# Row tiles transposed by VectorE in 32-row blocks, from quarter-row loads, in place of crossbar transposes

## The chip, the cores and the metric

The kernel runs on one core of a Trainium2 chip. Five engines work side by side, each through its own queue in the order in which its instructions were written: TensorE (PE; its weight loads are listed apart as PEld), VectorE (DVE), ScalarE (ACT), GpSimd (POOL) and SyncE (SP), which here only issues transfers. Semaphores tie the queues together. Matmul results land in PSUM, which has eight banks; GpSimd cannot reach it. The metric is the device time of one execution in microseconds (us). The median of two runs before is 370.06 us (369.67 and 370.45).

## The reference

x has 8 x 1024 rows of 768 float32 numbers, the weight matrix is 768 x 2304. Each row is divided by its root mean square, multiplied by gamma, and multiplied with the weights:

```python
def reference(x, gamma, w_qkv, eps):
    rms = np.sqrt(np.mean(x ** 2, axis=-1, keepdims=True) + eps)
    x_norm = x / rms * gamma
    return np.matmul(x_norm, w_qkv).astype(np.float32)
```

The output is 8 x 1024 x 2304 float32, 75.5 MB, x is 25.2 MB, the weights are 7.1 MB.

## The kernel before, in words

The 8192 rows are 64 tiles of 128 rows. TensorE contracts over partitions, so a tile of x must lie with its 768 columns on the partitions: six blocks (KO = 6) of 128 columns.

Tiles 0 to 3 take a plain way. x is cast to bfloat16 (`cast`), turned by TensorE (`tr`), copied out of PSUM (`cp`) and multiplied with the weights (`mm`, six matmuls of 512 columns for each output piece). The row factor 1/rms comes in when the result is taken out (`evac`). The weights are multiplied with gamma and cast in the meantime (`conv`). `gamma_in` turns gamma itself by a tiny float32 matmul (L482).

Tiles 4 to 63 are taken in pairs, p = 2 to 31: two row tiles by 768 output columns (c = 0, 1, 2) are a 2 x 2 by 2 x 2 block product, done with seven products in place of eight (Strassen's scheme in Winograd's form). The halves of the contraction are the first and last three of the six blocks of columns. The pieces are:

- `load_x`: one transfer for a tile, 3 KB for each partition.
- `pstat`, `prms`, `precip`: ScalarE squares a tile and adds along the row (L567, an ACTIVATE and a read of the accumulator); one root (L571) and one reciprocal (L576) serve a pair.
- `pcast` (L581): VectorE multiplies by 1/rms and casts to float16.
- `pxbar` (L585): a crossbar transpose, issued by SyncE, gives the tile `xT`.
- `osum` (L599): four sums and differences of half tiles for each pair, on GpSimd but for the first ones.
- `quad`, `tsum`: the eight weight operands in float16 for each c, made once, scaled by a bound on the column block (`bound`, `fold`, `bound_tr`, `bound_top`, `bound_all`, `scales`).
- `product` (L619): three matmuls of 384 columns. Seven products for each p and c go into three PSUM banks a, b, c.
- `hold` (L628 on ScalarE, L626 on VectorE), `join` (L637, VectorE) and `last` (L641, ScalarE): holds copy a partial sum out of a bank so that a further product can be added on top of it in the same bank; joins add a bank to a held part and write the output tile `ot`; last writes the fourth quarter. Product 6 goes into bank a after hold "p1" has read product 1; product 3 into bank c after hold "p5".
- `pstore` (L647): the output of a tile's 768 columns goes to memory.

The order is written out by hand. Each entry has a due time; all entries are sorted by it and issued in that order, so the due time sets the place in every engine's queue and nothing else. PLAN lists the first part: the weights, tiles 0 to 3, and pairs 2 to 11. HEAD_END (135.62) is the due time at which pair 12 begins. From pair 12 on the order is regular: one slot is three matmuls (SLOT = 0.4875 us), a column c takes seven slots, a pair 21. `when(u, ...)` places an operation u slots after the column's start; products 1, 5, 2, 6, 3, 7, 4 stand at 0, 1, 2, 4, 5, 10, 13, so the last two fall between those of the next column. Loads, square sums, casts and transposes of a pair stand many slots ahead of its first product, and are placed differently for even and odd pairs.

Tiles come from pools of a fixed number of buffers: nine for x, four for casts, ten for xT, twelve for outputs of 1024 columns, eight PSUM banks. An operation that wants a buffer waits until the earlier user is done with it.

Of the kernel before, what the change touches and what calls it, by code (L numbers as in the profile page):

```python
# [15 lines left out]
HEAD_END = 135.62  # L16
# [3 lines left out]
    (0.000, "load_x", 2), (4.040, "cast", 2, "DVE"), (4.041, "load_x", 0), (5.030, "cast", 0, "DVE"),  # L20
    (5.031, "stat", 2), (5.530, "recip", 2), (5.531, "gamma_in"), (5.532, "idle", 6, 512), (5.533, "tr", 2),
    (5.670, "tr", 0), (6.230, "cp", 0, "DVE"), (6.231, "stat", 0), (6.440, "cp", 2, "ACT"), (6.441, "load_x", 1),
    (6.442, "load_w", 3), (6.820, "cast", 1, "DVE"), (7.460, "tr", 1), (7.461, "load_w", 4),
    (7.480, "conv", 3, 4, "DVE"), (8.141, "conv", 4, 5, "DVE"), (8.142, "mm", 2, 0, "4"), (8.143, "load_w", 2),
    (8.801, "conv", 2, 3, "DVE"), (8.802, "load_w", 0), (8.803, "load_x", 3), (8.804, "cp", 1, "ACT"),
    (9.371, "bound", 0, 1, "DVE"), (9.372, "mm", 0, 0, "4"), (9.373, "mm", 2, 0, "5"), (9.374, "load_w", 1),
    (9.375, "mm", 0, 0, "5"), (9.376, "mm", 1, 0, "5"), (9.377, "mm", 1, 0, "4"), (9.574, "mm", 0, 0, "3"),
    (9.575, "load_w", 7), (9.576, "load_w", 5), (9.790, "mm", 1, 0, "3"), (11.111, "cast", 3, "DVE"),
    (11.112, "load_w", 6), (11.113, "stat", 1), (11.114, "conv", 0, 0, "ACT"), (11.115, "mm", 2, 0, "3"),
    (11.116, "conv", 0, 1, "POOL"), (11.117, "mm", 1, 0, "01"), (11.393, "mm", 0, 0, "01"), (11.394, "stat", 3),  # L30
    (11.395, "load_w", 9), (11.825, "tr", 3), (11.826, "conv", 1, 2, "DVE"), (13.092, "conv", 7, 4, "ACT"),
    (13.093, "conv", 7, 5, "POOL"), (13.094, "mm", 1, 0, "2"), (13.095, "mm", 2, 0, "012"), (13.205, "mm", 0, 0, "2"),
    (13.932, "mm", 2, 512, "45"), (14.364, "mm", 1, 512, "45"), (14.365, "load_w", 8), (14.413, "conv", 5, 1, "POOL"),
    (17.054, "conv", 9, 2, "POOL"), (17.055, "bound", 0, 0, "DVE"), (17.734, "conv", 9, 3, "POOL"),
    (17.735, "cp", 3, "DVE"), (17.736, "evac", 2, 0, "ACT"), (17.737, "mm", 0, 512, "54"),
    (17.738, "conv", 5, 0, "ACT"), (17.739, "mm", 3, 512, "45"), (18.414, "conv", 8, 0, "POOL"),
    (18.415, "mm", 2, 512, "01"), (18.416, "mm", 1, 512, "01"), (18.417, "recip", 1), (18.418, "evac", 1, 0, "DVE"),
    (18.419, "recip", 3), (18.420, "conv", 6, 3, "ACT"), (18.421, "conv", 6, 2, "DVE"),
    (18.422, "bound", 1, 0, "ACT"), (18.423, "load_w", 10), (18.424, "mm", 0, 512, "01"),
    (18.425, "mm", 0, 512, "23"), (18.426, "mm", 1, 512, "23"), (18.427, "mm", 2, 512, "23"),  # L40
    (18.428, "mm", 3, 512, "01"), (18.429, "evac", 1, 512, "ACT"), (18.430, "bound", 0, 2, "DVE"),
    (18.431, "recip", 0), (18.432, "fold", 0), (18.714, "conv", 8, 1, "ACT"), (19.494, "bound", 1, 1, "ACT"),
    (19.495, "bound_tr", 0), (19.496, "evac", 0, 0, "DVE"), (19.497, "mm", 2, 1024, "23"),
    (19.498, "mm", 0, 1024, "23"), (19.499, "bound_top", 0), (19.665, "bound_all", 0), (19.785, "mm", 2, 1024, "01"),
    (19.786, "load_x", 5), (21.094, "pstat", 5), (21.095, "mm", 3, 1024, "01"), (21.096, "evac", 0, 512, "DVE"),
    (21.097, "mm", 1, 1024, "01"), (21.098, "scales", 0), (21.099, "quad", 0, "b12", "DVE"),
    (21.100, "conv", 10, 5, "POOL"), (21.101, "conv", 10, 4, "POOL"), (22.064, "bound", 1, 2, "ACT"),
    (22.065, "mm", 0, 1024, "01"), (22.066, "quad", 0, "b22", "DVE"), (22.067, "load_w", 11),
    (22.068, "mm", 2, 1024, "45"), (22.069, "mm", 3, 1024, "45"), (22.535, "quad", 0, "b11", "DVE"),
    (23.275, "conv", 11, 0, "DVE"), (23.276, "load_x", 4), (23.705, "tsum", 0, "t3", "DVE"), (23.706, "load_w", 13),  # L50
    (24.405, "fold", 1), (24.406, "conv", 13, 5, "POOL"), (24.407, "pstat", 4), (24.408, "mm", 3, 512, "23"),
    (24.409, "mm", 0, 1024, "45"), (24.410, "mm", 1, 1024, "23"), (24.555, "evac", 3, 512, "DVE"),
    (24.556, "load_w", 15), (24.634, "conv", 11, 1, "ACT"), (24.635, "mm", 3, 1024, "23"),
    (24.636, "mm", 3, 0, "012345"), (25.215, "evac", 2, 512, "DVE"), (25.216, "load_x", 6), (25.396, "bound_tr", 1),
    (25.397, "prms", 2), (25.875, "precip", 2), (25.876, "mm", 1, 1024, "45"), (25.948, "mm", 2, 1536, "01"),
    (25.949, "load_x", 7), (25.950, "conv", 13, 4, "POOL"), (26.380, "mm", 2, 1536, "45"),
    (26.381, "conv", 15, 3, "POOL"), (26.382, "load_w", 12), (26.383, "bound_top", 1), (26.384, "conv", 15, 5, "DVE"),
    (26.455, "tsum", 0, "t1", "DVE"), (26.812, "bound_all", 1), (26.813, "conv", 15, 4, "ACT"),
    (26.932, "mm", 0, 1536, "01"), (26.933, "evac", 2, 1024, "ACT"), (26.934, "evac", 3, 1024, "ACT"),
    (27.363, "mm", 1, 2048, "345"), (27.691, "mm", 0, 1536, "45"), (27.692, "evac", 1, 1024, "ACT"),  # L60
    (27.693, "pcast", 4), (27.705, "pcast", 5), (27.706, "load_w", 14), (28.608, "conv", 12, 3, "POOL"),
    (29.635, "conv", 14, 0, "POOL"), (29.636, "tsum", 0, "t2", "DVE"), (29.637, "mm", 3, 1536, "45"),
    (29.638, "mm", 3, 1536, "01"), (29.639, "pxbar", 5), (29.640, "mm", 1, 1536, "01"), (29.641, "pstat", 6),
    (29.642, "pstat", 7), (29.643, "scales", 1), (29.644, "evac", 3, 0, "DVE"), (29.645, "mm", 1, 1536, "45"),
    (29.849, "mm", 3, 2048, "345"), (29.850, "conv", 12, 2, "ACT"), (30.177, "mm", 2, 2048, "345"),
    (30.334, "prms", 3), (30.335, "bound", 2, 1, "DVE"), (30.504, "mm", 3, 1536, "23"),
    (30.584, "conv", 14, 1, "ACT"), (31.615, "precip", 3), (31.616, "evac", 0, 1024, "ACT"),
    (31.617, "conv", 14, 2, "POOL"), (31.618, "mm", 1, 1536, "23"), (31.619, "mm", 2, 2048, "012"),
    (31.715, "osum", 2, "s1", "DVE"), (31.716, "mm", 1, 2048, "012"), (32.085, "pcast", 6),
    (32.086, "quad", 1, "b11", "ACT"), (32.814, "evac", 2, 2048, "ACT"), (32.815, "pcast", 7),  # L70
    (32.816, "quad", 0, "b21", "POOL"), (32.817, "mm", 3, 2048, "012"), (32.818, "pxbar", 4),
    (33.185, "osum", 2, "s2", "DVE"), (33.186, "load_x", 8), (33.187, "load_x", 10), (33.188, "mm", 0, 1536, "23"),
    (33.189, "mm", 2, 1536, "23"), (33.645, "osum", 2, "s4", "POOL"), (33.646, "quad", 1, "b21", "DVE"),
    (33.647, "pxbar", 6), (33.648, "product", 2, 0, 2), (33.649, "evac", 3, 2048, "ACT"),
    (33.701, "product", 2, 0, 1), (34.245, "evac", 1, 2048, "DVE"), (34.246, "load_x", 9), (34.445, "pxbar", 7),
    (35.215, "quad", 1, "b12", "POOL"), (35.216, "evac", 2, 1536, "DVE"), (36.485, "quad", 1, "b22", "POOL"),
    (36.486, "product", 2, 1, 1), (36.487, "product", 2, 1, 2), (36.488, "bound", 2, 0, "ACT"),
    (36.489, "evac", 3, 1536, "DVE"), (36.490, "hold", 2, 0, "a", "p1", "ACT"), (36.491, "load_x", 11),
    (36.492, "load_x", 12), (36.535, "load_x", 13), (36.536, "hold", 2, 1, "a", "p1", "DVE"),
    (36.537, "bound", 2, 2, "ACT"), (36.538, "product", 2, 0, 5), (36.539, "join", 2, 0, 0, 0, "b", "p1"),  # L80
    (36.540, "product", 2, 0, 6), (36.541, "product", 3, 0, 1), (37.205, "product", 3, 1, 2),
    (37.206, "join", 2, 1, 0, 0, "b", "p1"), (37.294, "hold", 2, 0, "c", "p5", "ACT"),
    (37.794, "evac", 1, 1536, "ACT"), (37.795, "fold", 2), (37.796, "store", 2, 1, 1024, 1024),
    (37.797, "tsum", 1, "t1", "DVE"), (38.394, "evac", 0, 1536, "ACT"), (38.465, "osum", 2, "s3", "DVE"),
    (38.466, "bound_tr", 2), (38.994, "hold", 2, 0, "a", "u2", "ACT"), (38.995, "product", 2, 0, 3),
    (38.996, "tsum", 1, "t2", "DVE"), (38.997, "product", 2, 1, 5), (39.494, "hold", 2, 1, "c", "p5", "ACT"),
# [215 lines left out]
def kernel(  # L302
# [115 lines left out]

    HALF = {"A": (0, 4), "B": (4, KO)}

    def tr_half(t, h):
        k0, k1 = HALF[h]
# [315 lines left out]
```

## Time and profile before

| | |
|---|---|
| median of two runs | 370.06 us |
| profiled execution, whole | 371.79 us |
| its span, first to last instruction | 369.5 us |
| mean granted TensorE clock | 0.995 of full speed |
| operand sums on GpSimd (L599), 114 in three groups | mean 929 to 948 ns for 128 x 384 |
| square sums on ScalarE (L567), 60 | 837 ns and a 191 ns accumulator read |
| casts on VectorE (L581), 60 | 690 ns mean, 612 median |
| holds on ScalarE / VectorE | 213 of 580 ns / 57 of 616 ns |
| joins (L637), 270 | 613 ns |
| products' matmuls (L619), 1890 | listed with 326 ns, pipelined; one starts every 0.163 us |
| their weight loads | 98 ns |
| crossbar transposes, issue on SyncE | 60, median 1390 ns |
| other issues on SyncE, median | output stores 384 ns, x loads 550 ns |
| an x load / a transpose / an output store, from issue to landing | 5.9 / 5.2 / 5.2 us |
| packets | 89295, of which 52390 are under 512 B |

A group's line gives line, engine, operation, output and inputs by their names in the program, shape and count; then the busy time, the mean of one in ns, and the idle time before them with what ended it. A wait line gives who waited, for whom, the sum in us, the number of times and the longest. A line of the chain or the timeline gives start and length in us. A window's line gives the stretch, then busy time and count for each engine, the granted clock, the busy share of the transfer engines and GB/s. Durations of neighbouring instructions on one engine overlap, so what one costs is read from the starts.

### The profile page before, as it was taken

To read this page: it belongs to the slowest core of one execution; us is meant where nothing else is said; L and a number is where in the kernel's file an instruction comes from. 1 tells how busy PE (TensorE), PEld (TensorE's weight loads), DVE (VectorE), ACT (ScalarE), POOL (GpSimd) and SP (SyncE) were. 2 spreads that over 40 slices of the span, in tenths; PEclk is the share of its full clock that TensorE was granted. 3 is DMA by queue.
4 is the path that set the end of the run, shared out by engine and by line. 5 is a ranking of instruction groups with operands and counts; after the bars stand their busy time and mean duration, and the time that the engine had idled before them with its cause. 6 is when DMAs were issued, how large, how long until landed. Compare 5 with 4: busy or idle time off the path is not lost.

```text
span 369.5 us, 6553 instructions
## 1 busy us (share of the span) xinstructions
PE 345.3 (93%) x2045; PEld 200.2 (54%) x2047; DVE 261.5 (71%) x484; ACT 247.5 (67%) x502; POOL 126.2 (34%) x141
## 2 busy tenths in 40 slices
PE   5998999799989989889999999999999999999995
PEld 3444555465545545545656566565656656556663
DVE  3899978587557857657868576776868676776653
ACT  4798988476558767447585765757575776745453
POOL 0257734324214433333043342507070613343000
PEclk9999999999999999989999999999999999999999
DMA  7998999989999999999999999999999999786656
GB/s 256 392 387 218 268 398 267 333 264 326 265 394 365 342 323 350 274 364 353 390 328 410 293 402 347 403 300 391 330 382 312 359 335 360 286 259 244 248 227 245
DMA packets 89295, 119.98 MB, mean 325 GB/s; under 512 B 52390, under 2 KB 54188, under 8 KB 89260
## 3 DMA queue, kind: packets, MB, share of 16 engines
q1 hardware_dynamic: 89248, 119.56, 98.8%
q8 instruction: 16, 0.26, 0.3%
q14 instruction: 19, 0.16, 0.2%
q10 hardware_dynamic: 12, 0.00, 0.0%
HBM read 32.25 MB, written 75.50 MB: 292 GB/s over the span
## 4 chain that ended last, share of the span: by engine, by line
PE 59%; DMA 20%; ACT 7%; issue 5%; DVE 3%; SPq 3%; POOL 1%; ACTq 0%; DVEq 0%; POOLq 0%
PE pm L619 59%; DMA out_dram<-ot 11%; DMA wq<-in_w_qkv_dram 7%; ACT sq L567 3%; DVE ot L637 2%; ACT pp L628 2%; SPq L370 2%; ACT ot L641 1%; DMA xT<-xb 1%; SPq L585 1%; DVE xb L581 1%; POOL wq L551 1%; POOL w_b L385 1%; ACT sq L509 0%; SPq L647 0%
## 5 line engine op out<-in xcount | busy, mean ns | idle before, releaser
L619 PE MATMUL pm<-wq,su 128*128 128x384 f16 x1080 | 207.1, 326 | 7.4 <-ACT pp L628 4.6
L637 DVE SCALAR_TENSOR_TENSOR ot<-pm,sc,pp 128x384 f32<-128x384 f32 x270 | 156.3, 613 | 70.5 <-PE pm L619 43.7
L628 ACT ACTIVATE pp<-pm,sc 128x384 f32<-128x384 f32 x213 | 121.1, 580 | 77.6 <-PE pm L619 76.1
L619 PE MATMUL pm<-wq,xT 128*128 128x384 f16 x810 | 161.8, 327 | 6.7 <-DVE ot L637 6.6
L619 PEld LDWEIGHTS <-su 128*128 128x128 f16 x1080 | 105.3, 98 | 80.8 <-issue 11.0
L619 PEld LDWEIGHTS <-xT 128*128 128x128 f16 x810 | 79.5, 98 | 62.1 <-issue 10.9
L599 POOL TENSOR_TENSOR su<-xT 128x384 f16<-128x384 f16 x55 | 50.9, 946 | 176.1 <-DMA xT<-xb 139.4
L641 ACT ACTIVATE ot<-pm,sc 128x384 f32<-128x384 f32 x90 | 51.8, 577 | 32.1 <-PE pm L619 27.9
L626 DVE TENSOR_SCALAR pp<-pm,sc 128x384 f32<-128x384 f32 x57 | 35.1, 616 | 23.2 <-PE pm L619 23.2
L567 ACT ACTIVATE sq<-x_t 128x768 bf16<-128x768 f32 x60 | 50.2, 837 | 0.5
L581 DVE TENSOR_SCALAR xb<-x_t,rstd 128x768 f16<-128x768 f32 x60 | 41.2, 690 | 1.1 <-DMA xT<-xb 0.5
L599 POOL TENSOR_TENSOR su<-su,xT 128x384 f16<-128x384 f16 x29 | 27.5, 948 | 12.5 <-DMA xT<-xb 9.9
L599 POOL TENSOR_TENSOR su<-xT,su 128x384 f16<-128x384 f16 x30 | 27.9, 929 | 3.8 <-DVE su L599 1.6
L449 PE MATMUL pm<-w_b,xT 128*128 128x512 bf16 (+1 forms) x118 | 25.7, 369 | 1.6 <-POOL w_b L385 1.2
L449 PEld LDWEIGHTS <-xT 128*128 128x128 bf16 x120 | 11.7, 100 | 13.2 <-issue 3.4
L385 POOL TENSOR_SCALAR w_b<-wq,g_sb 128x512 bf16<-128x512 f32 (+1 forms) x14 | 11.6, 837 | 20.0 <-DMA wq<-in_w_qkv_dram 20.0
L567 ACT ACTIVATION_READ_ACCUMULATOR sq<-x_t 128x1 f32 x60 | 11.5, 191 | 0.0
L571 ACT ACTIVATE rms<-ssq,eps_sb 128x2 f32<-128x2 f32 x30 | 8.8, 292 | 0.2
L557 DVE TENSOR_TENSOR wq<-wq 128x1152 f16<-128x1152 f16 x11 | 8.1, 747 | 0.0
L506 DVE TENSOR_REDUCE bnd<-w_b 128x1 f32<-128x1536 bf16 x4 | 7.0, 1753 | 0.9 <-POOL w_b L385 0.4
L509 ACT ACTIVATE sq<-w_b 128x1536 bf16<-128x1536 bf16 x5 | 7.4, 1480 | 0.3
L383 ACT ACTIVATE w_b<-wq,g_sb 128x512 bf16<-128x512 f32 (+1 forms) x9 | 6.0, 669 | 1.9 <-DMA wq<-in_w_qkv_dram 1.8
(47 smaller groups left out, 67.2 us busy)
## 6 DMA issues: line engine op xcount, KB each, us to landing
out_dram<-ot SPq DMA_DIRECT2D x178, 384.0 KB, 5.2
x_t<-in_x_dram SPq DMA_DIRECT2D x64, 384.0 KB, 5.9
wq<-in_w_qkv_dram SPq DMA_DIRECT2D x10, 512.0 KB, 9.3
out_dram<-ot SPq DMA_DIRECT2D x8, 512.0 KB, 8.5
wq<-in_w_qkv_dram SPq DMA_DIRECT2D x4, 256.0 KB, 6.9
xT<-xb SPq DMA_TRANSPOSE x60, 5.2
wq<-in_w_qkv_dram SPq DMA_DIRECT2D x2, 384.0 KB, 9.8
out_dram<-ot SPq DMA_DIRECT2D x4, 192.0 KB, 2.3
```

The lines of the kernel that those rows point to most:

```text
L385: nc.gpsimd.tensor_scalar(out=o, in0=i, scalar1=g, scalar2=1.0, op0=mult, op1=mult)
L449: nc.tensor.matmul(out=PM[t, n0][:, :nl], lhsT=XT[t][:, ko, :], rhs=w_b[:, ko, n0:n0 + nl], start=(b == 1), stop=(b == KO))
L557: (nc.vector if eng == "DVE" else nc.gpsimd).tensor_tensor(out=new_quad(c, q), in0=i0, in1=i1, op=sub)
L567: nc.scalar.activation(out=sq, in_=X[t], func=AF.Square, accum_out=SS[p][:, t % 2:t % 2 + 1])
L571: nc.scalar.activation(out=r, in_=SS[p], func=AF.Sqrt, scale=inv_k, bias=eps_sb)
L581: nc.vector.tensor_scalar(out=XB[t], in0=X[t], scalar1=SS[t // 2][:, t % 2:t % 2 + 1], scalar2=None, op0=mult)
L599: (nc.vector if eng == "DVE" else nc.gpsimd).tensor_tensor(out=block(p, q), in0=block(p, x), in1=block(p, y), op=op)
L619: nc.tensor.matmul(out=PB[k][:, :CW], lhsT=block(p, a)[:, ko, :], rhs=WQ[c, b][:, ko, :], start=(first and ko == 0), stop=(ko == KO // 2 - ...
L626: nc.vector.tensor_scalar(out=o, in0=pb, scalar1=SC[c], scalar2=None, op0=mult)
L628: nc.scalar.activation(out=o, in_=pb, func=AF.Copy, scale=SC[c], bias=0.0)
L637: nc.vector.scalar_tensor_tensor(out=result(p, c, i, j), in0=PB[p, c, bank][:, :CW], scalar=SC[c], in1=PART[p, c, held], op0=mult, op1=add)
L641: nc.scalar.activation(out=result(p, c, 1, 0), in_=PB[p, c, "a"][:, :CW], func=AF.Copy, scale=SC[c], bias=0.0)
```

## The change: what it does

- x of tiles 4 to 63 comes as quarter rows (`load_g`): four transfers for each tile, packets of 768 B. On partition 32 g + i lie, side by side, the g-th quarters of rows i, 32 + i, 64 + i, 96 + i (index m).
- The square sums are taken for each quarter row: `pstat(t, h)` makes two of the four 192-column sums of a tile. The four quarters of a row lie on four partitions; `psum_k` adds them with one float32 matmul against a 0/1 matrix `same_row` for each pair, and hands the sums to all four partitions. `prms` and `precip` then work on eight columns.
- `pcast` is a multiplication of two tensors, on GpSimd but for two tiles in the first part.
- `pturn` is a VectorE transpose in 32 x 32 blocks. Two neighbouring float16 numbers are treated as one 32-bit word, so 384 words per partition give the whole tile. Partition q then holds columns 6 q to 6 q + 5 of all 128 rows, with the two numbers of a word next to each other: the weight operand that TensorE loads steps over every other half word.
- The weights are loaded to match (row 6 q + ko on partition q), gamma comes straight into that layout (`gamma_in` goes), the two halves of the contraction are the even and odd ko, and the first tiles' cast writes its columns in that order.
- Crossbar transposes, and some functions without a caller, are removed.
- PLAN is written anew: tiles 5 and 4 are loaded early, other operations change engine, HEAD_END is 142.52. In the regular part even and odd pairs now have the same offsets, and the hold "p5" of the third column is on VectorE too.

```diff
-HEAD_END = 135.62
+HEAD_END = 142.52
...
-    g6 = singles.tile([KO, P], f32)
-    nc.scalar.dma_start(out=g6, in_=gamma.rearrange("(ko p) -> ko p", p=P))
+    gam = singles.tile([P, KO], f32)
+    nc.scalar.dma_start(out=gam, in_=gamma.rearrange("(p ko) -> p ko", ko=KO))
...
+    row_sel = singles.tile([P, B], f32)
+    nc.vector.tensor_reduce(out=row_sel, in_=ident_f.rearrange("p (g i) -> p i g", g=G), axis=mybir.AxisListType.X, op=add)
+    same_row = singles.tile([P, P], f32)
+    nc.vector.tensor_copy(out=same_row.rearrange("p (g i) -> p g i", g=G), in_=row_sel.unsqueeze(1).to_broadcast([P, G, B]))
...
-    wv = w_qkv.rearrange("(ko p) n -> p ko n", p=P)
+    wv = w_qkv.rearrange("(p ko) n -> p ko n", ko=KO)
...
-        copy(eng, XB[t], X[t])
+        copy(eng, XB[t].rearrange("p (ko q) -> p q ko", ko=KO), X[t].rearrange("p (q ko) -> p q ko", ko=KO))
...
-        k0, n0 = KO // 2 * (q[1] == "2"), 2 * CW * c + CW * (q[2] == "2")
-        return w_b[:, k0:k0 + KO // 2, n0:n0 + CW]
+        s, n0 = int(q[1] == "2"), 2 * CW * c + CW * (q[2] == "2")
+        return w_b.rearrange("p (b s) n -> p s b n", s=2)[:, s, :, n0:n0 + CW]
...
-    def pstat(t):
+    def load_g(t):
+        X[t] = xin.tile([P, G, K // G], f32, name="x_t")
+        xs = xf[t * P:(t + 1) * P, :].rearrange("(m i) (g k) -> g m i k", i=B, g=G)
+        for m in range(G):
+            nc.sync.dma_start(out=X[t][:, m, :], in_=xs[:, m])
+
+    def pstat(t, h):
         p = t // 2
         if p not in SS:
-            SS[p] = stats.tile([P, 2], f32, name="ssq2")
-        sq = junk.tile([P, 2 * K], bf16, name="sq")[:, :K]
-        nc.scalar.activation(out=sq, in_=X[t], func=AF.Square, accum_out=SS[p][:, t % 2:t % 2 + 1])
+            SS[p] = stats.tile([P, 2 * G], f32, name="ssq2")
+        sq = junk.tile([P, 2 * K], bf16, name="sq")[:, :K // G]
+        for m in (2 * h, 2 * h + 1):
+            i = G * (t % 2) + m
+            nc.scalar.activation(out=sq, in_=X[t][:, m, :], func=AF.Square, accum_out=SS[p][:, i:i + 1])
+
+    def psum_k(p):
+        ps = psum.tile([P, 2 * G], f32, name="pm")
+        nc.tensor.matmul(out=ps, lhsT=same_row, rhs=SS[p], start=True, stop=True)
+        SS[p] = ps
...
-    def pcast(t):
-        XB[t] = xbp.tile([P, K], f16, name="xb")
-        nc.vector.tensor_scalar(out=XB[t], in0=X[t], scalar1=SS[t // 2][:, t % 2:t % 2 + 1], scalar2=None, op0=mult)
-
-    def pxbar(t):
-        XT[t] = xTp.tile([P, KO, P], f16, name="xT")
-        nc.sync.dma_start_transpose(out=XT[t], in_=XB[t])
+    def pcast(t, eng):
+        XB[t] = xbp.tile([P, G, K // G], f16, name="xb")
+        r = SS[t // 2][:, G * (t % 2):G * (t % 2 + 1)]
+        (nc.vector if eng == "DVE" else nc.gpsimd).tensor_tensor(
+            out=XB[t], in0=X[t], in1=r.unsqueeze(2).to_broadcast([P, G, K // G]), op=mult)
+
+    def pturn(t):
+        o = xTp.tile([P, H, P], f32, name="xT")
+        nc.vector.transpose(out=o.rearrange("p b (m i) -> p m b i", i=B),
+                            in_=XB[t].rearrange("p m k -> p (m k)").bitcast(f32).rearrange("p (m j b) -> p m b j", m=G, j=B))
+        XT[t] = o.rearrange("p b q -> p (b q)").bitcast(f16).rearrange("p (b q s) -> p s b q", s=2, q=P)
...
-                odd = p % 2
                 for i in range(2):
                     t = 2 * p + i
-                    when((-96, -110)[odd] + 7 * i, load_x, t)
-                    when((-64, -78)[odd] + 7 * i, pstat, t)
-                    when((-45, -57)[odd] + 4.5 * i, pcast, t)
-                    when((-42, -54)[odd] + 4.5 * i, pxbar, t)
-                when((-54.5, -68)[odd], prms, p)
-                when((-46, -58)[odd], precip, p)
+                    when(-72 + 7 * i, load_g, t)
+                    when(-46 + 7 * i, pstat, t, 0)
+                    when(-43 + 7 * i, pstat, t, 1)
+                    when(-30 + 7 * i, pcast, t, "POOL")
+                    when(-22.3 + 7 * i, pturn, t)
+                when(-33.5, psum_k, p)
+                when(-32.5, prms, p)
+                when(-31, precip, p)
...
-            when(2.1, hold, p, c, "c", "p5", "DVE" if c < 2 else "ACT")
+            when(2.1, hold, p, c, "c", "p5", "DVE")
```

## The prediction, made before any run of the change

> **What bounds the kernel now.** I read the page's busy times first, then the chain that ended last, then who waited for whom, and last the windows, in which matmuls can be counted and held against the written order.
>
> ```profile
> PE 345.3 (93%) x2045; PEld 200.2 (54%) x2047; DVE 261.5 (71%) x484; ACT 247.5 (67%) x502; POOL 126.2 (34%) x141
> ...
> PE 59%; DMA 20%; ACT 7%; issue 5%; DVE 3%; SPq 3%; POOL 1%; ACTq 0%; DVEq 0%; POOLq 0%
> ```
>
> TensorE is busy nearly throughout, yet 20% of the chain is transfers. The waits say where they come in:
>
> ```profile
> DVE ot L637 <- DMA out_dram<-ot: 19.5, 22, 2.9
> ...
> PE pm L619 <- DVE ot L637: 6.6, 9, 1.9
> ...
> PE pm L619 <- ACT pp L628: 4.6, 10, 0.5
> ```
>
> A join on VectorE waits until an old output tile has been stored; TensorE then waits for that join's bank. All 22 of these waits lie between 30 and 165 us. The windows (us, then busy time and count of TensorE, weight loads, VectorE, ScalarE, GpSimd, then clock, DMA share, GB/s):
>
> ```profile
> 0.00:65.00 65.00, 57.90 (x314) 30.60 (x317) 53.05 (x105) 53.66 (x101) 29.25 (x35) 1.00 0.98 313
> 0.00:150.00 150.00, 136.17 (x781) 76.17 (x784) 111.05 (x210) 110.84 (x221) 57.45 (x65) 1.00 1.02 321
> ...
> 190.00:320.00 130.00, 126.68 (x775) 75.54 (x774) 93.51 (x174) 88.28 (x189) 49.17 (x55) 1.00 1.06 349
> 340.00:350.00 10.00, 10.00 (x64) 5.99 (x62) 6.20 (x12) 5.20 (x11) 0.00 (x0) 1.00 0.61 243
> ```
>
> A run of 108 matmuls in the chain takes 17.73 us, so one takes 0.1626 us when nothing waits (the last one's 0.17 tail taken off). The plan has 775 matmuls before pair 12, the first pair of the regular part; 781 had run by 150 us, so pair 12 began at 149.0. Its due time was 135.62, and the first load goes out at 0.73: **12.7 us late**. At 65 us the kernel had run 314 matmuls, about where it was due at 62: 2 to 3 us late. So some 10 us were lost between 65 and 149, in the waits for stores. After pair 12, 2047 - 775 = 1272 matmuls need 206.8 us; the last ended at 365.6, so 9.8 us were lost there too, and 3.9 us of last evacuation and store make the span of 369.5.
>
> In the regular part (190 to 320) 775 matmuls take 130 us, 10.57 us for a pair's 63 where 10.24 would do: 0.3 us a pair. The chain shows why:
>
> ```profile
> 209.43 0.83 ACT L567 ACTIVATE sq<-x_t 128x768 bf16<-128x768 f32 x1
> 210.16 0.19 ACT L567 ACTIVATION_READ_ACCUMULATOR sq<-x_t 128x1 f32 x1
> 210.38 0.84 ACT L567 ACTIVATE sq<-x_t 128x768 bf16<-128x768 f32 x1
> 211.13 0.19 ACT L567 ACTIVATION_READ_ACCUMULATOR sq<-x_t 128x1 f32 x1
> 211.23 0.56 ACT L641 ACTIVATE ot<-pm,sc 128x384 f32<-128x384 f32 x1
> 211.69 0.57 ACT L628 ACTIVATE pp<-pm,sc 128x384 f32<-128x384 f32 x1
> ```
>
> Two whole sums of squares stand ahead of a last and a hold, and product 6 waits for that hold. Starts matter here, not durations: a hold frees ScalarE after 0.47, an accumulator read lets a hold follow after 0.10, another sum after 0.22.
>
> **What goes.** 60 crossbar transposes. In 340 to 350 there are none: 243 GB/s at a share of 0.61 is 398 GB/s at full share. In 190 to 320, 349 GB/s moved 45.4 MB; 25 tiles' transposes are 5.0 of it (0.197 MB each), the other 40.4 MB take 101.5 us at 398, and the remaining 28.5 us are 1.1 us a transpose. 60 of them are some 66 us of transfer time, 1.4 us each of SyncE's queue, too. The 41 us of casts on VectorE (L581) go as well, but for two.
>
> **What comes, per pair of 63 matmuls.**
>
> x in quarter rows: 8 issues where there were 2, packets of 768 B where there were 3 KB. SyncE: 8 x 0.43 + 6 stores x 0.38 = 5.7 us of 10.2, against 2 x 0.43 + 2 x 1.39 + 6 x 0.38 = 5.9 before; no gain, no loss. A tile's 393 KB take 1.0 us at 398 GB/s. No row has such packets: nothing more at one end, at the other twice the time (a transpose, with 870 small packets, pays 1.1 us for half the bytes). I take 1.3: of the 66 us that the transposes free, 60 x 0.3 = 18 are spent again; at twice the time 60 of them are, and the queue is as full as before.
>
> Sums of squares: 8 of 192 columns for 2 of 768. From the starts: 0.73 for 768 is 0.64 + 0.09, so 192 take 0.25, then 0.22 and 0.10 around the reads: 0.82 for each half tile, 3.3 us a pair against 1.7. With nine holds and lasts at 0.49 and the root, ScalarE fills 8.0 of 10.2 us. The halves are due apart (slots 3, 6, 17, 20 of 21). The tightest place: hold at slot 19.35, half tile, last, hold: 19.35 + 1.0 + 1.7 + 1.0 + 1.2 = 24.25, needed at 25. It fits by 0.4 us, so most of the 0.3 us stall should go. I put the loss S at 0.1 a pair, 3 us in all; bounds 0 and, as before, 0.3 (10 us).
>
> GpSimd: two casts of 768. Its subtractions take 0.93 for 384 columns and 2.94 for 1152, 2.6 ns a column: 1.94 each. With four operand sums 7.6 of 10.2; the second cast ends at about slot 5.5, its transpose stands at 5.7 in VectorE's order. VectorE: a transpose of 384 words has no row; 0.35 (the quickest 384-column sum) and 1.75 (a reduction of 1536) bound it, I take 0.62, as any one-input row of its size. Twelve joins and holds at 0.573, two transposes, a reciprocal: 8.3 of 10.2. The Trainium skill, "SBUF — State Buffer" (Door 1: The DMA port swizzle), says that reads which leave their 16-byte line pay; the transposes read words 12 bytes apart, and no run here shows it. By that rule VectorE would have perhaps 9.5 of 10.2, still hidden.
>
> Weight loads from xT now step over every other half word: 98 ns at best, twice that at worst, and 196 would stick out of a matmul's 163 by 33 ns, 27 us for 810. I take 98.
>
> **The new float32 product (psum_k)** is the one thing added to TensorE itself, 30 times. It stands in the queue ahead of all products and waits for the last square sum. Nearest rows (busy us, mean ns, idle before):
>
> ```profile
> L528 PE MATMUL pm<-btop,ones 1*128 1x1 bf16 x3 | 0.5, 173 | 0.0
> ...
> L482 PE MATMUL pm<-ident_f,g 6*128 6x6 f32 x1 | 0.2, 241 | 2.3 <-DMA g<-in_gamma_dram 2.3
> ...
> L482 PEld LDWEIGHTS pm<-ident_f,g 6*128 6x128 f32 x1 | 0.2, 177 | 2.3 <-POOL ones L492 2.3
> ```
>
> L528's follower starts 0.11 after it (21.14, 21.25): the low end. The only float32 row, L482, takes 177 for weights and 241: 0.42 when nothing covers its weights, which is the case behind a wait; a full 128 x 128 product could be twice that, 0.84. I take 0.42. The plan already leaves 0.13 after ten of them. Net 30 x 0.42 - 10 x 0.13 = 11.3 us. The rule against this change is in "FP8 and Floating Point Precision" (TensorE Precision Notes): a true float32 product makes four passes. Four passes at the 0.163 of an ordinary matmul would be 0.65 and the total 7 us more; no row here shows it.
>
> Strided casts, the selector matrix and gamma by column touch only the first microseconds, under the wait for x (2.16 us of VectorE at 1.7 to 3.9): nothing, or 1 us, inside L below.
>
> **The sum.** The changed plan puts pair 12 at 142.52, with 789 TensorE instructions before it (12 of the 30 psum_k). Start 0.73: 143.25. After it 2076 - 789 - 18 = 1269 products' matmuls x 0.1626 = 206.3. Tail 3.9. Together 353.5. Lateness L of the first part: 2 to 3 us without the store waits, and more work on ScalarE: 4; bounds 0 and 12.7. 353.5 + 4 + 11.3 + 3 = **371.8** against the span of 369.5, 2.3 more. That execution took 371.79 in all, 1.7 over the median of 370.06; I add the 2.3 to the median: **372.4**. The plan's later start and the float32 products eat what the transfers give.
>
> **Rivals.**
> - Faster, 0.22: psum_k at 0.11 (2.0), L 2, S 0: 353.5 + 4.0 = 357.5, 358 us. For it: L528; nothing else lies on TensorE. Against: float32.
> - Slower by ScalarE, 0.10: if reads of the accumulator cost their recorded 354 + 191 (1536 to 768 columns give 0.84 ns a column and 194 fixed), a half takes 1.1 us. The chain above then ends at 25.2, and the second half before psum_k at about slot 9.9 instead of 8.4, with psum_k at 9. That is 0.4 a pair in psum_k's wait and 0.3 in product 6: 22 us for S's 3, 391 us. It decides from 0.95 us a half.
> - The float32 product at its upper end, 0.12: 30 x 0.42 more, 385 us.
> - No relief, 0.07: small x packets refill the queue, L and S as before: 353.5 + 12.7 + 11.3 + 10, 388 us. The change then isn't what its transfers promise.
> - Strided weights (399 us) or a GpSimd cast at 4 us, from the 1371 ns row of 256 columns: 11.9 of 10.7 us a pair (406 us); 0.07.
> - My forecast 0.42, its own range 364 to 381.
>
> A measurement of this kernel tells some 2% (7.4 us) from no change. Faster 0.22. Slower: 0.10 + 0.12 + 0.07 + 0.07 and 0.06 from the forecast's upper end, 0.42. Within 0.36. For eight in ten the range takes in half of the fast case, the float32 and ScalarE ones: 359 to 391.
>
> **What to look for after.** No wait of L637 for stores; DMA share below 0.95 after 60 us; pair 12 near 147 (count 789); TensorE's idle time before psum_k and its span; 3.3 us of ScalarE starts per pair; PEld from xT still 98; GpSimd casts near 1.9. I am wrong if psum_k is far from 0.42, if holds wait behind square sums, or if the head loses more than 8 us again.

## The result, and the profile after

The changed kernel takes **486.27 us** (median of two runs, 484.96 to 487.59) against 370.06 before: a ratio of 1.314 (95% interval 1.298 to 1.330). The forecast was 372.4, with a range up to 391. Its profiled execution has a span of 483.2 us at a mean granted clock of 0.936. First the busy times and the chain that ended last, from the page of the changed kernel:

```profile
PE 379.0 (78%) x2106; PEld 213.7 (44%) x2106; DVE 293.8 (61%) x524; ACT 276.1 (57%) x824; POOL 208.7 (43%) x199
...
DMA 51%; PE 18%; SPq 17%; DVE 4%; issue 4%; ACT 4%; POOL 2%; DVEq 0%; ACTq 0%; POOLq 0%
```

TensorE fell from 59% of the chain to 18%. Transfers went from 20% to 51%, and SyncE's queue, which issues them, from 3% to 17%. The waits of the changed kernel (us in total, times, longest) say which transfers:

```profile
ACT sq L568 <- DMA x_t<-in_x_dram: 69.8, 97, 3.4
...
DVE ot L637 <- DMA out_dram<-ot: 46.1, 22, 7.7
...
PE pm L572 <- ACT sq L568: 35.7, 16, 2.7
```

The square sums now wait for x itself, which they hardly did before (all 60 of them together had 0.5 us of idle time in front). The joins' waits for stores, which were to go, grew from 19.5 to 46.1 us. A window of the regular part, with the columns of the windows shown for the kernel before, seems to contradict this:

```profile
190.00:320.00 130.00, 105.76 (x612) 60.93 (x610) 78.88 (x142) 77.15 (x244) 57.82 (x54) 0.96 0.61 229
```

612 matmuls instead of 775, and the transfer engines at a share of only 0.61, against 1.06 before. The kernel waits for transfers while, on average, four tenths of the transfer engines' time is free. That average is the trap of this case. The chain of the changed kernel (start, length, what) shows the loop that each pair runs through:

```profile
281.95 0.57 SPq L559
...
282.57 0.83 SPq L559
...
283.45 0.58 SPq L559
...
284.08 7.67 DMA x_t<-in_x_dram
...
291.83 0.10 ACT sq L568
...
292.33 0.39 PE pm L572 x2
292.72 2.53 PE pm L619 x9
...
295.27 0.59 ACT pp L628
...
296.01 0.57 SPq L559
```

The last quarter load of the pair, 98 KB, takes 7.67 us from its issue. After it come the square sum, psum_k, nine products, a hold, a store, and the next issue 14.06 us after the first. psum_k starts at 263.04, 278.08, 292.33, 306.59 and 320.83 us: **14.45 us a pair**, where 10.57 was measured before. The lower granted clock is not what lengthens a pair: of two neighbours, one at a clock of 0.88 and one at 0.98, both take 14.2 to 14.3 us:

```profile
292.33:306.59 14.26, 12.32 (x66) 6.90 (x66) 8.34 (x15) 8.16 (x27) 6.43 (x6) 0.88 0.59 222
306.59:320.83 14.24, 10.80 (x65) 6.30 (x65) 8.41 (x15) 8.27 (x27) 6.43 (x6) 0.98 0.58 220
```

### The profile page after: what moved, and what is told of

Read it like the earlier page. It is cut to its first block, busy times and chain, and to the rows that moved or that the text cites. A ratio compares the mean times of both kernels' runs of the same rounds, so it can differ in the third digit from the quotient of the medians.

```text
span 483.2 us, 7420 instructions
## 1 busy us (share of the span) xinstructions
PE 379.0 (78%) x2106; PEld 213.7 (44%) x2106; DVE 293.8 (61%) x524; ACT 276.1 (57%) x824; POOL 208.7 (43%) x199
## 4 chain that ended last, share of the span: by engine, by line
DMA 51%; PE 18%; SPq 17%; DVE 4%; issue 4%; ACT 4%; POOL 2%; DVEq 0%; ACTq 0%; POOLq 0%
DMA x_t<-in_x_dram 28%; DMA out_dram<-ot 20%; PE pm L619 17%; SPq L559 13%; DMA wq<-in_w_qkv_dram 3%; DVE ot L637 3%; SPq L647 2%; ACT sq L568 1%; PE pm L572 1%; POOL su L608 1%; ACT ot L641 1%; ACT pp L628 1%; SPq L469 1%; POOL xb L588 1%; DVE xT L593 1%
## 5 line engine op out<-in xcount | busy, mean ns | idle before, releaser
L619 PE MATMUL pm<-wq,su 128*128 128x384 f16 x1080 | 222.2, 342 | 26.5 <-DVE pp L626 13.1
L637 DVE SCALAR_TENSOR_TENSOR ot<-pm,sc,pp 128x384 f32<-128x384 f32 x270 | 157.8, 609 | 112.4 <-DMA out_dram<-ot 46.1
L619 PE MATMUL pm<-wq,xT 128*128 128x384 f16 x810 | 170.7, 339 | 14.0 <-DVE ot L637 13.8
L588 POOL TENSOR_TENSOR xb<-x_t,rstd 128x768 f16<-128x768 f32 x58 | 85.4, 1473 | 214.6 <-DVE rstd L582 166.1
L628 ACT ACTIVATE pp<-pm,sc 128x384 f32<-128x384 f32 x179 | 102.7, 576 | 75.4 <-PE pm L619 60.9
L568 ACT ACTIVATE sq<-x_t 128x192 bf16<-128x192 f32 x240 | 86.6, 361 | 73.1 <-DMA x_t<-in_x_dram 69.8
L626 DVE TENSOR_SCALAR pp<-pm,sc 128x384 f32<-128x384 f32 x91 | 55.8, 613 | 27.6 <-PE pm L619 27.4
L568 ACT ACTIVATION_READ_ACCUMULATOR sq<-x_t 128x1 f32 x240 | 45.1, 188 | 0.0
L593 DVE STREAM_TRANSPOSE xT<-xb 128x384 f32<-128x384 f32 x60 | 41.6, 694 | 0.0
L572 PE MATMUL pm<-ssq,same_row 128*128 128x8 f32 x60 | 11.3, 261 | 37.9 <-ACT sq L568 35.7
L572 PEld LDWEIGHTS pm<-ssq,same_row 128*128 128x128 f32 x60 | 10.4, 206 | 46.8 <-ACT sq L568 42.3
L400 POOL TENSOR_SCALAR w_b<-wq,gam 128x512 bf16<-128x512 f32 (+1 forms) x14 | 11.2, 810 | 31.3 <-DMA wq<-in_w_qkv_dram 31.3
```

What stands on the lines that cost most here:

```text
L568: nc.scalar.activation(out=sq, in_=X[t][:, m, :], func=AF.Square, accum_out=SS[p][:, i:i + 1])
L572: nc.tensor.matmul(out=ps, lhsT=same_row, rhs=SS[p], start=True, stop=True)
L588: (nc.vector if eng == "DVE" else nc.gpsimd).tensor_tensor(out=XB[t], in0=X[t], in1=r.unsqueeze(2).to_broadcast([P, G, K // G]), op=mult)
L593: nc.vector.transpose(out=o.rearrange("p b (m i) -> p m b i", i=B), in_=XB[t].rearrange("p m k -> p (m k)").bitcast(f32).rearrange("p (m j ...
L619: nc.tensor.matmul(out=PB[k][:, :CW], lhsT=block(p, a)[:, ko, :], rhs=WQ[c, b][:, ko, :], start=(first and ko == 0), stop=(ko == KO // 2 - ...
L626: nc.vector.tensor_scalar(out=o, in0=pb, scalar1=SC[c], scalar2=None, op0=mult)
```

## Why a small load takes so long: the theories

Every quarter load reads, in one transfer, a quarter of each row of a tile: from DRAM 4 column quarters, in each 32 rows (the g and i of `load_g`), in each 192 neighbouring numbers. The outermost dimension of that pattern has 4 entries. The load before had 128 rows outermost.

- **Theory N (narrow):** a transfer is spread over as many of the 16 transfer engines as its outermost dimension allows; here four, and always the same four. At the 398 GB/s of the prediction one engine moves 24.9 GB/s. x of a pair, 0.786 MB, keeps four engines busy for 7.9 us, and their part of the outputs (2.36 MB over 16 engines) for 5.9 us: 13.8 us a pair, while twelve engines are idle more than half the time.
- **Theory Q (queue):** eight issues a pair on SyncE, behind stores that wait for their data, send the loads off too late.
- **Theory P (packets):** packets of 768 B are slow by themselves.

The Trainium skill, "DMA: Bandwidth & Descriptors" (Why a DMA increments its semaphore by 16 and not by 1), states the rule that N needs: a transfer uses the largest number of engines, 16 at most, that divides the slowest dimension of both patterns, and from such a queue always the lowest-numbered ones. The prediction did not weigh it. The runs below agree with it for 2, 4 and 16; the trace does not number the engines.

## The experiments

**1. The same quarters, cut another way (e1_wide).** Each load now reads one column quarter of all 128 rows, with 32 rows outermost; bytes, packet size, number of issues and what lands where are the same.

```diff
-xs = xf[t * P:(t + 1) * P, :].rearrange("(m i) (g k) -> g m i k", i=B, g=G)
-for m in range(G):
-    nc.sync.dma_start(out=X[t][:, m, :], in_=xs[:, m])
+xs = xf[t * P:(t + 1) * P, :].rearrange("(m i) (g k) -> g i m k", i=B, g=G)
+for g in range(G):
+    nc.sync.dma_start(out=X[t][B * g:B * (g + 1), :, :], in_=xs[g])
```

> The changed kernel with one edit: a tile's four loads are cut by column quarter (32 partitions, all four row groups) and not by row group; same bytes, same 768 B packets, same four issues, same places. The source pattern then begins with a dimension of 32 and not of 4. Theory N (the quarter loads run on 4 of the 16 transfer engines, which carry 7.9 us of x and 5.9 us of outputs a pair): back to 360-385 us, about 10.6 us a pair. Theory Q (the loads stand too late in SyncE's queue, behind stores) and theory P (768 B packets are slow): above 470 us as before the edit.

Measured: **369.16 us**, ratio to the kernel before 0.9996 (0.9974 to 1.0019). From the page of this run, and its window of the regular part:

```profile
PE 346.5 (94%) x2104; PEld 206.6 (56%) x2106; DVE 291.8 (79%) x524; ACT 272.1 (74%) x824; POOL 209.1 (57%) x199
...
PE 85%; DMA 7%; DVE 3%; ACT 2%; SPq 1%; issue 1%; ACTq 0%; DVEq 0%
```

```profile
190.00:320.00 130.00, 130.00 (x817) 79.82 (x816) 103.20 (x188) 100.53 (x326) 80.69 (x76) 1.00 0.92 313
```

One rearrangement of the source takes away 117 us, and TensorE is busy 130.00 of 130 us. A quarter load lands after a median of 3.3 us. The joins' waits for stores, and the issues of quarter loads in the changed kernel and in this run (shortest, median and longest in ns):

```profile
DVE ot L637 <- DMA out_dram<-ot: 4.0, 6, 1.1
...
L559 SPq DMA_DIRECT2D x_t<-in_x_dram x240: 528/861/3063, 1.2 to 442.9; - x120
...
L559 SPq DMA_DIRECT2D x_t<-in_x_dram x240: 311/462/2302, 1.2 to 321.7; - x120
```

Packets of 768 B and eight issues a pair are harmless in this kernel: P and Q are out as the cause of the 486 us.

**2. Loads 24 slots earlier (e2_early).** The changed kernel, one number changed.

```diff
-when(-72 + 7 * i, load_g, t)
+when(-96 + 7 * i, load_g, t)
```

> The changed kernel with the regular part's loads 24 slots (11.7 us) earlier, nothing else. Theory Q: the loop from issue to landing to psum_k to the next issue is cut, the regular part runs at about 10.6 us a pair and the whole at 400-425 us (the first part keeps its loss). Theory N: four transfer engines still carry 13.8 us a pair, so 13.8 to 14.4 a pair and 465-490 us.

Measured: 486.02 us. The last load of a pair now goes off some 15 us ahead of its psum_k, 8.2 in the changed kernel, and a pair still takes 14.5 us. A loop that is only started too late would have gained; a full engine doesn't.

**3. Two engines instead of four (e9_two_engines).** The changed kernel with each quarter load issued as two halves, two column quarters each.

```diff
-nc.sync.dma_start(out=X[t][:, m, :], in_=xs[:, m])
+for h in range(2):
+    nc.sync.dma_start(out=X[t][64 * h:64 * h + 64, m, :], in_=xs[2 * h:2 * h + 2, m])
```

> The changed kernel with each quarter load issued as two halves, so that the outermost dimension of the source is 2 and not 4. Theory N (a load runs on as many transfer engines as that dimension has entries): x of a pair, 0.786 MB, on two engines at 24.9 GB/s each is 15.8 us, and their share of the outputs 5.9 us, so 21.7 us a pair against 14.3 with four, some 7.4 us more for each of about 28 pairs: 670 to 720 us in all. If the packets of 768 bytes or SyncE's issues were the bound: SyncE spends 16 x 0.54 = 8.6 us a pair on loads, with 2.5 us of stores 11 us a pair, below the present 14.3, so 480 to 500 us.

Measured: 748.13 us, above N's range and far from the other answer. Starts of psum_k in this run's timeline of TensorE:

```profile
201.31 0.28 PE L573 MATMUL pm<-ssq,same_row 128*128 128x8 f32 x2
...
297.28 0.28 PE L573 MATMUL pm<-ssq,same_row 128*128 128x8 f32 x2
```

Four pairs in 95.97 us, 24.0 us a pair, where N expected 21.7. The packets in the trace explain most of the rest. I counted the packets of each size that are under way at the same time, from 190 to 320 us of the span:

```
run               x packets (768 B)              output packets
                  mean    number under way       (3 KB), mean
e1_wide           42 ns   8 or more: 28% of time    134 ns
changed kernel    36 ns   exactly 4: 31%, more: 13% 124 ns
e9_two_engines    37 ns   exactly 2: 52%, more: 11% 125 ns
e12_two_queues    36 ns   exactly 4: 29%, more: 12% 123 ns
```

This is N seen directly: in the narrow runs the commonest number under way, whenever there is any, is the outermost dimension (above it, neighbouring packets' records overlap). The output packets show that it is always the same engines: in the changed kernel 12 or 13 of them are under way for 24% of the time and exactly 4 for 16%, in e9 14 or 15 for 17% and exactly 2 for 9%. That is what a store spread over all 16 gives if the same four, or two, always carry x: its other packets go ahead, and the share of the busy engines comes last. And 768 B in 36 to 37 ns are some 21 GB/s, not 24.9. A pair has 1024 packets of x and 768 of outputs: with two engines 512 x 37 ns + 48 x 125 ns = 24.9 us (24.0 measured), with four 256 x 36 + 48 x 124 = 15.2 us (14.45 measured).

**4. Two queues (e12_two_queues).** The changed kernel with half of its quarter loads issued by ScalarE.

```diff
-nc.sync.dma_start(out=X[t][:, m, :], in_=xs[:, m])
+(nc.sync if m < 2 else nc.scalar).dma_start(out=X[t][:, m, :], in_=xs[:, m])
```

> The changed kernel with two of the four quarter loads of a tile issued by ScalarE and two by SyncE, the source pattern left as it is. Theory N with the same four engines serving both queues: the four still carry x and a quarter of the outputs, 13.8 us a pair, so 480 to 490 us, with up to 10 us more where ScalarE's work waits behind its 0.5 us issues. If each queue had four engines of its own, the two halves would run on eight: x of a pair 3.9 us and outputs 5.9 us on each, 9.8 us a pair, under TensorE's 10.4, so 370 to 385 us.

Measured: 491.82 us, with x packets still four at a time. Another queue brings no other engines, and halving SyncE's issues helps nothing.

**5. The narrow pattern in the kernel before (e4_narrow_before).** Its whole-tile load with rows in the order of their number modulo 4: packets of 3 KB, two issues a pair, 4 outermost.

```diff
-nc.sync.dma_start(out=X[t], in_=xf[t * P:(t + 1) * P, :])
+nc.sync.dma_start(out=X[t], in_=xf[t * P:(t + 1) * P, :].rearrange("(i g) k -> g i k", g=4))
```

> The kernel before with one edit: an x load takes its 128 rows in the order 0, 4, 8, ... so that its source pattern begins with a dimension of 4; packets of 3 KB, one issue a tile and all places as before. Left out: the rows of a tile are not put back in order at the output. Theory N: 7.9 us of x, 5.9 of outputs and about 2.2 of transposes a pair on four engines, 14 to 16 us a pair, 470-530 us. Theories Q and P: as the kernel before, 366-378 us.

Measured: 565.34 us, above the 470 to 530 expected. The pattern alone, without any other part of the change, costs some 196 us (368.81 on the same chip). The window shows the average share at 1.10 here, about as before, at six tenths of the matmuls:

```profile
190.00:320.00 130.00, 92.24 (x484) 50.70 (x483) 61.33 (x112) 59.20 (x124) 26.61 (x29) 0.86 1.10 219
```

16.9 us a pair. Four engines' x (64 packets x 125 ns = 8 us) and outputs (6 us) make 14; the rest is probably with the crossbar transposes, whose 256 B packets took a mean of 103 ns instead of 28. How a busy engine holds a transpose up was not tried.

**6. Four loads a tile in the kernel before (e5_quarters_before).** The load cut into four of 192 columns of all 128 rows: packets of 768 B on 16 engines.

```diff
-nc.sync.dma_start(out=X[t], in_=xf[t * P:(t + 1) * P, :])
+for m in range(4):
+    nc.sync.dma_start(out=X[t][:, 192 * m:192 * (m + 1)], in_=xf[t * P:(t + 1) * P, 192 * m:192 * (m + 1)])
```

> The kernel before with each x load cut into four issues of 768 B packets, all with a leading dimension of 128. Theory N: 368-380 us, only SyncE's six more issues a pair (2.3 us) and some packet overhead. Theory P: 450 us or more. Theory Q, as far as it is the number of issues on SyncE: 390-430 us.

Measured: 410.54 us, ratio 1.113 (1.109 to 1.117); N, which had expected 368 to 380, is not the whole story in this kernel. The chain of this run shows x loads queued one behind the other on SyncE:

```profile
228.46 0.43 SPq L371
...
228.94 0.43 SPq L371
...
229.41 0.43 SPq L371
...
229.89 0.43 SPq L371
...
230.36 2.24 DMA x_t<-in_x_dram
```

So the number of issues probably matters where the same queue also issues two transposes a pair, 1.4 us each. In the wide-load kernel these are gone, and the same eight issues cost nothing visible. Packet size and issue count were both changed here, so their shares of the 42 us stay open; the chain speaks for the issues.

**7. What psum_k costs (e8_no_row_sum).** The wide-load kernel without the product that adds the four quarters.

```diff
-ps = psum.tile([P, 2 * G], f32, name="pm")
-nc.tensor.matmul(out=ps, lhsT=same_row, rhs=SS[p], start=True, stop=True)
-SS[p] = ps
+pass
```

> The wide-load kernel without the float32 product that adds the four quarters' square sums (the root is taken of each quarter's own sum, so the scale of each quarter row is that of the quarter alone, and not the row's). It prices that product: at 0.14 us each, as the period of 10.38 us a pair says, 30 of them are 4.2 us and the time is 364 to 366 us; at the 0.42 us of the prediction, 12.6 us and 356 to 357 us; if TensorE had room for it, 369 us.

Measured: 364.66 us (363.06 to 365.71 in four executions), 4.5 less than the wide-load kernel's 369.16. The timeline of the wide-load kernel has the same price in its starts:

```profile
252.72 0.65 PE L619 MATMUL pm<-wq,su 128*128 128x384 f16 x3
253.20 0.28 PE L572 MATMUL pm<-ssq,same_row 128*128 128x8 f32 x2
253.34 0.65 PE L619 MATMUL pm<-wq,xT 128*128 128x384 f16 x3
...
263.58 0.28 PE L572 MATMUL pm<-ssq,same_row 128*128 128x8 f32 x2
```

The next product starts 0.14 us after psum_k, and 63 x 0.1626 + 0.14 = 10.38 us is the distance of the two psum_k. One call shows as two instructions.

**8. Sums in float16 (e10_half_sums).** The wide-load kernel with the square sums and `same_row` in float16.

```diff
-same_row = singles.tile([P, P], f32)
+same_row = singles.tile([P, P], f16)
...
-SS[p] = stats.tile([P, 2 * G], f32, name="ssq2")
+SS[p] = stats.tile([P, 2 * G], f16, name="ssq2")
...
```

> The wide-load kernel with the quarters' sums of squares and the matrix that adds them in float16 instead of float32 (sums of 192 squares, far below the largest float16 here; each is rounded to some 1 part in 4000). Theory: the float32 product costs 0.14 us of TensorE's stream because it is two passes with a weight load each; in float16 it is one pass, two records fewer per pair become one, and the period falls from 10.38 to 10.30 us a pair: 30 x 0.07 = 2 us, so 366 to 368 us. If the price sits in the wait for the square sums and not in the passes, 369 us; if it is gone altogether, 364.7 us as in the run without it.

Measured: **366.07 us**, ratio to the kernel before 0.9908 (0.9888 to 0.9929): 0.9% quicker than the kernel before, and quicker than the wide-load kernel. One instruction remains, and its follower starts 0.03 us after it:

```profile
250.34 0.65 PE L620 MATMUL pm<-wq,su 128*128 128x384 f16 x3
250.82 0.17 PE L573 MATMUL pm<-ssq,same_row 128*128 128x8 f16 x1
250.85 0.65 PE L620 MATMUL pm<-wq,xT 128*128 128x384 f16 x3
```

So 0.11 of the 0.14 us went, more than the half I had expected: 30 x 0.11 = 3.3 us, measured 3.1.

**9. The first part: three tries (e6_plain_cast, e7_loads_first, e11_first_part).** In the wide-load kernel the regular part runs without a stall, yet the total only equals the kernel before. Pair 12 (count 801, psum_k shows twice) begins at 154.5 us, 11.3 after its due 143.25. Two groups of this run stand out against the kernel before, where a cast took 0.56 us and the transposes of the first tiles waited 2.1 us:

```profile
L404 DVE CAST xb<-x_t 128x768 bf16<-128x768 f32 x4 | 7.3, 1926 | 4.1 <-DMA x_t<-in_x_dram 4.1
...
L428 PE MATMUL pm<-ident,xb 128*128 128x128 bf16 x24 | 3.3, 310 | 12.7 <-DVE xb L404 8.3 <-DVE rstd L422 4.4
```

e6 writes the casts in plain order and lets the weight load step over six numbers instead:

```diff
-copy(eng, XB[t].rearrange("p (ko q) -> p q ko", ko=KO), X[t].rearrange("p (q ko) -> p q ko", ko=KO))
+copy(eng, XB[t], X[t])
...
-nc.tensor.transpose(out=PT[t][:, ko, :], in_=XB[t][:, ko * P:(ko + 1) * P], identity=ident)
+nc.tensor.transpose(out=PT[t][:, ko, :], in_=XB[t].rearrange("p (q ko) -> p ko q", ko=KO)[:, ko], identity=ident)
```

> The wide-load kernel (369.2 us) with the first four tiles cast in plain order and the order of k taken over by TensorE's weight load, which then steps by 6 elements. Its first part is 6 us later than in the kernel before, and each of its four casts took 1.87 to 2.08 us, against 0.56 before: 4 x 1.35 = 5.4 us of VectorE in the first 16 us. Theory C (the strided casts made the first part late): 364 to 366 us, and pair 12 begins near 151 rather than 155. Theory O (the order of the first loads did: SyncE issues eight quarter loads, 4.3 us, ahead of the second tile and the weights): 368 to 370 us, because VectorE waits for data anyway. A weight load of 16-bit numbers 12 bytes apart that is slow would show as a mean over 98 ns in the first 16 us; 24 of them cannot cost 1 us.

Measured: 369.38 us (ratio 1.0011, 0.9981 to 1.0042), as without it. By 20 us 51 matmuls have started instead of 38, by 60 us 219 instead of 225: the head start is lost again on the way.

e7 adds a new order of the first loads in PLAN (`load_x` 0, 1, 3 and eight `load_w` ahead of `load_g` 5 and 4, whose sums, casts and transposes come some 10 us later).

> The kernel with plain casts, and in the first 20 us the loads of tiles 0, 1 and 3 and of the weights issued ahead of the eight quarter loads of pair 2; that pair's square sums, casts and transposes are moved behind them in the plan. Theory O: the first weight product, at 16.1 us in the wide-load kernel and at 9.3 us in the kernel before, comes near 10 us, pair 12 begins 4 to 6 us earlier, and the time is 361 to 364 us. Theory C: no more than 1 us off the run with plain casts. A third way: the weights' transfers are the bound of the first 50 us, and pair 2 then comes too late to fill TensorE's gaps between 30 and 50 us; the time is that of the plain casts or up to 4 us over it.

Measured: 371.96 us (1.0068, 1.0041 to 1.0095), 2.6 over the run with plain casts. The time is that of the third way; that the weights' transfers are the bound there is not shown by it.

e11 is e10 with plain casts and four entries of PLAN changed to thin out VectorE's dense stretch from 41 to 56 us (`evac 3, 1536` to ScalarE, `tsum 2, t1` later, `osum 3, s2` and `s4` earlier).

> The same, with the plain casts of the first four tiles and four entries of the first part's plan moved: one eviction at 46.6 us goes from VectorE to ScalarE, one sum of weights of the third chunk behind the products of the second, and pair 3's two sums of row blocks ahead of two sums of weights. In the wide-load kernel VectorE is busy without a gap from 41 to 56 us, and TensorE waits for it 3 us between 49 and 53 us. If VectorE's order there sets the end of the first part, 1.3 to 3 us are gained over the run with float16 sums: 363 to 366 us. If the weights' loads and their conversion do, as the runs with plain casts and with moved loads suggest, less than 1 us: 366 to 368 us.

Measured: 367.48 us (0.9958, 0.9932 to 0.9983), no gain over e10. The stretch is on the chain of the wide-load kernel, but thinning it out in this way gains nothing. The chain of the wide-load kernel there:

```profile
46.73 0.66 DVE ot L463
47.40 0.82 DVE wq L550
48.22 0.47 DVE su L608
48.69 1.62 DVE wq L550
```

What makes the first part late stays open. It is not the casts alone, and the one other order of the first loads that was tried did not help; between 20 and 60 us VectorE is busy for 37.5 of 40 us in the wide-load kernel (36.1 before) and for 33.5 in e6, which is no quicker. TensorE's clock is at half for 3.4 us from 53.3 us in the wide-load kernel, which is 1.7 us at most, and e11, without such a stretch in its first part, is no quicker than e10 either.

## Why the prediction was wrong

**The step that failed** is "x in quarter rows": "A tile's 393 KB take 1.0 us at 398 GB/s ... I take 1.3". It priced bytes over all 16 engines and weighed only the size of the packets. The load runs on four engines: 512 packets / 4 x 36 ns = 4.6 us of these four for each tile, and a part of the outputs on top, 14.45 us a pair in all where TensorE needs 10.24. The upper bound, twice 1.0, was as wrong, because both ends shared the unsaid premise of 16 engines. The rival "no relief" had the queue as full as before; in truth four engines were full, and twelve were idle for more than half of the time. No row of the trace before could show it, since all its loads of x and of the weights began with 128 rows; the pattern in `load_g` did, and I read it for its packet length alone.

The sum, term by term (us; psum_k of the first twelve pairs counts into the lateness of the runs):

| term | forecast | wide loads | changed kernel |
|---|---|---|---|
| start of pair 12 by plan | 143.25 | 143.25 | 143.25 |
| lateness of the first part (L) | 4 | 11.3 | 58.1 |
| 1269 matmuls | 206.3 | 206.3 | 206.3 |
| psum_k | 11.3 | 2.5 (18 x 0.14) | in the next |
| stalls after pair 12 (S), in the runs what is left over | 3 | 0.7 | 71.6 |
| tail | 3.9 | 3.9 | 3.9 |
| span | 371.8 | 368.0 | 483.2 |

Pair 12 of the changed kernel begins at 201.4 us (798 matmuls by 200; its first is the 802nd); from there 483.2 - 201.4 = 281.8 us remain, 71.6 more than matmuls and tail. Nearly all of it lies between the 18 psum_k that follow: 17 distances of 14.38 us on average from 206.82 to 451.25, where 10.24 would do, are 70 us. With wide loads the forecast of 371.8 is near, but that is luck, by errors that cancel: psum_k 8.8 too dear (7.1 with the twelve that L holds in the run), S 2.3 too high, L 7.3 too low.

- **psum_k**: 0.42 was the price behind a wait with no cover. In the stream its weights load beside the products, and it is 0.14. Behind a wait, in the changed kernel, the next product starts 0.25 us after it (292.33 and 292.58). The prediction's other figure, four passes at the 0.163 of an ordinary matmul, took the price of 384 columns for a product of 8. The Trainium skill's "four passes" themselves ("FP8 and Floating Point Precision", TensorE Precision Notes) can't be seen here: the trace lists two instructions a call and doesn't say what passes one holds.
- **L**: I expected lateness to go with the stores' waits. They did shrink (19.5 to 4.0 us in the wide-load kernel), but that kernel is 8.5 us behind its own plan by 60 us, against 3.2 for the kernel before, and the plan itself is 6.9 us longer. These eat what the freed transfers bring.
- **Transfers**: right where the loads are wide: share 0.92 instead of 1.06 and no stall in the regular part, 9.8 us of stalls there became 0.7.
- **SyncE**: "no gain, no loss" holds with wide loads; in the changed kernel issues are longer (median 861 ns against 462).
- **ScalarE**: a half tile is 0.84 from its start to that of the next instruction (251.93 and 252.77 in the wide-load kernel; 0.82 forecast), and the rival of 391 us has nothing for it. **GpSimd's** casts took 1.47 us, not 1.94. **VectorE's** transposes took 0.694 us, not 0.62. By the 16-byte lines of the Trainium skill's "SBUF — State Buffer" (Door 1: The DMA port swizzle) the prediction had VectorE at perhaps 9.5 us instead of 8.3, 0.6 more for each transpose; the trace shows 0.07 more, and as no run has the words in order, it stays open whether that is their price. **Weight loads** of every other half word: 100 ns in the wide-load kernel, 98 taken.
- **What to look for**: "DMA share below 0.95" came true in a kernel 30% slower. As a sign of relief it was badly chosen.

## What to carry to other kernels

Before a transfer is priced in bytes, read its access pattern from the outside: here an outermost dimension of 2 or 4 put it on two or four transfer engines, and 32 or 128 on all, which was worth more than long packets (565.34 us with 3 KB and 4 outermost, 369.16 with 768 B and 32). A mean busy share of the transfer engines says nothing about the fullest of them: with waits for transfers and a share well under 1, look at how many packets are under way at once. Where a rearrangement is free to choose its outer dimension, split the load along the other one.

## What the runs showed of the hardware that was not expected

- Loads of this pattern had four engines in all, whether one queue or two issued them (491.82 us with SyncE and ScalarE).
- An issue onto few engines is itself slower: the shortest took 503 ns with 2 entries outermost and 522 to 536 ns with 4, in both kernels and on both queues, against 328 to 332 ns with 128 and 311 ns with 32.
- A float32 product of 128 x 128 x 8 is two instructions, 0.14 us in a running stream and 0.25 us behind a wait; in float16 one, 0.03 us in the stream.
- A VectorE cast that writes 16-bit results 256 bytes apart takes 1.93 us for 768 columns, 3.4 times the 0.56 us of plain order.
